# Head norms and memory softmax worked in place in PSUM, and an instruction index that goes back when a leading stream ends

## The chip, the cores and the metric

The kernel runs on one core of one Trainium2 chip. The metric is the device time of one execution in microseconds (us). Engines are named as in the profile: PE is the matrix engine (PEld its weight loads), DVE the vector engine, ACT the scalar engine, POOL the general-purpose engine, SP the engine that issues the transfers. SBUF is the working memory, PSUM the eight banks of 512 fp32 words per partition into which PE writes.

## The reference: two layers of a decoder trunk

Inputs are `x` (512 tokens of 1024), 256 memory tokens and the weights, all fp32. Each layer normalises `x`, projects it, runs three branches, gates them, concatenates them, projects back and adds.

```python
# layer 0:  A chunked spatial gating | B differential attention (8 heads x 2 maps of 32) | M memory attention
# layer 1:  C conformer convolution (31 taps) | D sparse attention (8 heads of 64, 2 groups) | M memory attention
q = rope_partial(rms_norm(q, qnorm), pos)        # per head: a "head norm", with or without rotation
def memory_attention(q, mem_n, w_kv, qnorm, knorm):
    k, v = jnp.split(mem_n @ w_kv, 2, axis=-1)
    q, k = rms_norm(q.reshape(..., 4, 64), qnorm), rms_norm(k.reshape(..., 4, 64), knorm)
    p = jax.nn.softmax(jnp.einsum('bshd,bmhd->bhsm', q, k) * 64 ** -0.5, axis=-1)
    return jnp.einsum('bhsm,bmhd->bshd', p, v)
```

## The kernel before

Tokens are cut into four tiles of 128. Products that need fp32 accuracy are made from two fp32r halves (high and low), three matmuls per product (`mm3`, L396 to L398). Each weight unit (128x1024) arrives by DMA, ACT writes its high half (`split`, L376) and POOL its low half (L377, POOL). Outputs that become matmul operands are split by ACT and DVE (L376, L377).

**Head norms.** `head_norm` (L488) serves memory queries and keys of both layers (`m_query`, `mem_kv`) and queries and keys of branch D (`d_q`, `d_kv`). The projection `p` lies in a PSUM bank. ACT squares it into the SBUF tile `sq`; DVE sums per head (L494); `rstd` takes two POOL instructions (L370, L372). Meanwhile DVE multiplies `p` by gain (L498) or gain times cosine (L501) into SBUF, over `sq`, makes the sine part `u` (L503) and adds it in two pieces (L504, L505). When `r` is there, `to_queries` multiplies by it in SBUF (L521) or `to_keys` does so into a doubled tile (L511), and PE transposes. `b_qk` does the same for branch B with its own lines (L873 to L883; L883 multiplies by `r`). From L504, L881, L511, L521 and L883 on, all tensors are in SBUF. Two token tiles of `b_qk`, and two of the layer-0 memory queries, share one PSUM bank; the others have a bank each.

**Memory softmax.** `m_attn` (L586) treats two heads at once, in one bank `s`: DVE takes the maximum (L600), ACT writes the exponentials to SBUF `e` (L603), DVE scales head 0 (L572) and POOL head 1 (L570) in place, PE transposes, ACT and DVE split, PE multiplies by the values (L582 to L584). There are 16 such steps, 8 in each layer.

**Compressed values and gates of D.** `d_cmp` copies a 64x64 PSUM result to SBUF by ACT (L1111) and spreads it with eight DVE copies (L1115); `m_q1` turns a tanh into a gate on DVE (L1134), once for each token tile.

**What sets the order.** The kernel emits all instructions once, and a scheduler at build time fixes each engine's queue: among the instructions that it holds ready it takes the one with the lowest index, and the index counts up as instructions are emitted. A block `high_priority(offset=n)` numbers its instructions from the current index minus n and at its normal end puts the index back, so that they use up no numbers. Streams are generators: `merge` interleaves a leading one with a filling one, and `ahead(g, n)` (L719) runs each step of the leading one in such a block. A generator that ends raises StopIteration inside the block. The block is then left by an exception, and the index isn't put back: it stays lower by n for all that follows. There are four leading streams: `m_attn` of layer 0 (n = 1000), `m_attn` of layer 1 (1000), `d_cmp` (100), `d_attn` (100). The convolution taps (`c_taps`, L1243; DVE L1260 and, for one channel tile, ACT L1257 with POOL L1258) are numbered 2000 higher than their place, so that they fill gaps; they read what `c_glu` projects (L1235, L1238). Dependences hold whatever the index. For PSUM they are kept by bank: a read of one half of a bank waits for a write of its other half that was emitted before it, and a write for such a read.

Banks and pages are handed out by the kernel at emission. Projections take banks of kind "d": six at first, three from the differential attention of layer 0 on, four in the projections of D.

## Time and profile before

| | |
|---|---|
| three timed runs | 733.96, 735.17 (median), 738.78 us |
| the profiled execution | 736.76 us |
| its span, first to last instruction | 734.7 us (2.06 us lie outside) |
| mean granted PE clock | 0.979 |
| busy: PE, PEld, DVE, ACT, POOL | 673.6, 571.1, 534.5, 366.9, 388.5 us |
| chain that ended last | PE 59%, DVE 23%, POOL 7%, ACT 4%, issue 4%, DMA 2% |

An engine's busy time is the time in which at least one of its instructions runs. A matmul's end is modelled and successive ones overlap, so a mean of 380 ns for one with 512 columns stands beside starts 227 ns apart. The stages of the span: start to 16 us, projections and head norms of B to 132, attention of B with its filling projections to 290, memory attention 0 and the output projection to 345, layer-1 norm to 361, memory queries, first channel tiles and memory attention 1 to 440 (its last products come at 480), projections of D to 545, attention of D to the end. The granted clock is given as a share of 2.4 GHz; 0.5 is 1.2 GHz.

### The profile page before, as it was taken

What the parts mean: (1) busy time and instruction counts of PE and PEld (TensorE: products, weight loads), DVE (VectorE), ACT (ScalarE), POOL (GpSimd) and SP (SyncE); (2) the same over time, 40 slices, a digit from 0 to 9 for tenths busy, and PEclk for the clock granted to TensorE, in tenths of its full rate; (3) what the DMA queues carried; (4) which work ended last, traced back from release to release, by engine and by line L of the source; (5) the groups of instructions that cost most, each with busy time, mean ns of one, the idle gap of its engine ahead of it and who ended that gap; (6) DMA issues with size and microseconds to landing.
All of it is one profiled execution on the core that took longest, in us unless ns stands there. A gap on an engine that the chain in (4) does not pass through costs nothing.

```text
span 734.7 us, 10935 instructions
## 1 busy us (share of the span) xinstructions
PE 673.6 (92%) x3819; PEld 571.1 (78%) x3819; DVE 534.5 (73%) x1216; ACT 366.9 (50%) x819; POOL 388.5 (53%) x343
## 2 busy tenths in 40 slices
PE   4999999999999888999899899698697989989997
PEld 3789998788899767888787777586586878777885
DVE  4607787767867788952749939997959678888773
ACT  5344354555464664732534466432425566665651
POOL 3376985554366469524647389963625233511450
PEclk9999999999999999999999999999898999999999
DMA  8542254643231435222223111022211011110121
GB/s 307 162 143 73 69 148 111 186 115 119 72 116 59 143 115 200 76 71 58 92 86 118 56 58 58 29 90 83 83 34 58 29 58 31 63 52 1 58 72 72
DMA packets 22375, 66.55 MB, mean 91 GB/s; under 512 B 3504, under 2 KB 3760, under 8 KB 22320
## 3 DMA queue, kind: packets, MB, share of 16 engines
q1 hardware_dynamic: 22320, 65.86, 27.4%
q8 instruction: 30, 0.49, 0.3%
q14 instruction: 25, 0.20, 0.1%
HBM read 57.46 MB, written 2.10 MB: 81 GB/s over the span
## 4 chain that ended last, share of the span: by engine, by line
PE 59%; DVE 23%; POOL 7%; issue 4%; ACT 4%; DMA 2%; SPq 0%; POOLq 0%; DVEq 0%; ACTq 0%
PE banks L396 15%; PE banks L397 15%; PE banks L398 15%; PE banks L393 5%; DVE banks L1260 4%; PE banks L923 3%; DVE arena_r L377 2%; POOL arena_f L372 2%; POOL arena_r L377 2%; DMA arena_f<-in_wall_dram 2%; PE banks L1211 2%; ACT arena_r L376 2%; DVE arena_f L925 2%; PE banks L961 1%; POOL arena_f L1258 1%
## 5 line engine op out<-in xcount | busy, mean ns | idle before, releaser
L396 PE MATMUL banks<-arena_r 128*128 128x512 f32 (+2 forms) x784 | 293.5, 380 | 13.9 <-DVE arena_f L473 3.3
L397 PE MATMUL banks<-arena_r 128*128 128x512 f32 (+2 forms) x784 | 292.2, 374 | 4.2 <-POOL arena_r L377 3.1
L398 PE MATMUL banks<-arena_r 128*128 128x512 f32 (+2 forms) x784 | 290.7, 373 | 0.6 <-POOL arena_r L377 0.5
L377 POOL TENSOR_TENSOR arena_r<-arena_f,arena_r 128x1024 fp32r<-128x1024 f32 (+2 forms) x87 | 211.2, 2436 | 143.9 <-ACT arena_r L376 141.3
L396 PEld LDWEIGHTS banks<-arena_r 128*128 128x128 f32 x784 | 150.6, 193 | 40.3 <-ACT arena_r L376 5.2
L397 PEld LDWEIGHTS banks<-arena_r 128*128 128x128 f32 x784 | 150.4, 192 | 28.0 <-POOL arena_r L377 4.0
L398 PEld LDWEIGHTS banks<-arena_r 128*128 128x128 f32 x784 | 150.1, 192 | 24.7 <-POOL arena_r L377 1.4
L376 ACT ACTIVATE arena_r<-arena_f 128x1024 fp32r<-128x1024 f32 (+2 forms) x131 | 110.4, 854 | 80.8 <-PE banks L398 19.3
L393 PE MATMUL banks<-const,arena_f 128*128 128x128 f32 x507 | 83.5, 281 | 28.0 <-DVE arena_f L411 9.6
L393 PEld LDWEIGHTS banks<-const,arena_f 128*128 128x128 f32 x507 | 62.6, 146 | 39.0 <-DVE arena_f L411 10.1
L377 DVE TENSOR_TENSOR arena_r<-banks,arena_r 128x512 fp32r<-128x512 f32 (+1 forms) x112 | 67.0, 608 | 26.1 <-ACT arena_r L376 25.6
L376 ACT ACTIVATE arena_r<-banks 128x512 fp32r<-128x512 f32 (+1 forms) x112 | 57.8, 532 | 43.9 <-PE banks L393 27.1
L925 DVE CUSTOM_DVE_ANT_0 arena_f<-banks,const 128x512 f32<-128x512 f32 (+3 forms) x128 | 60.2, 484 | 21.1 <-PE banks L923 15.1
L372 POOL TENSOR_TENSOR arena_f<-arena_f,const 128x4 f32<-128x4 f32 (+3 forms) x60 | 68.6, 1146 | 3.6
L570 POOL TENSOR_SCALAR arena_f<-arena_f 128x256 f32<-128x256 f32 (+3 forms) x48 | 29.0, 609 | 74.2 <-DVE arena_f L1190 25.2
L1260 DVE SCALAR_TENSOR_TENSOR banks<-arena_f,const,banks 128x482 f32<-128x482 f32 (+14 forms) x90 | 66.0, 733 | 1.4
L954 ACT ACTIVATE arena_f<-arena_f 128x512 f32<-128x512 f32 (+3 forms) x64 | 35.8, 560 | 45.8 <-DVE arena_f L925 45.4
L923 PE MATMUL banks<-arena_r 128*128 128x512 f32 (+7 forms) x192 | 51.5, 345 | 4.2 <-DVE arena_f L925 4.1
L653 DVE TENSOR_TENSOR arena_f<-arena_f,banks 128x512 f32<-128x512 f32 x40 | 27.3, 684 | 29.0 <-PE banks L398 28.3
L1188 ACT ACTIVATE arena_f<-arena_f 128x512 f32<-128x512 f32 (+3 forms) x64 | 35.6, 558 | 24.2 <-DVE arena_f L925 24.2
L370 POOL TENSOR_SCALAR arena_f<-arena_f 128x4 f32<-128x4 f32 (+3 forms) x60 | 19.0, 317 | 47.9 <-DVE arena_f L494 15.8
L923 PEld LDWEIGHTS banks<-arena_r 128*128 128x128 f32 (+1 forms) x192 | 33.1, 193 | 9.0 <-DVE arena_f L925 5.9
(175 smaller groups left out, 847.0 us busy)
## 6 DMA issues: line engine op xcount, KB each, us to landing
arena_f<-in_wall_dram SPq DMA_DIRECT2D x88, 512.0 KB, 3.3
arena_r<-arena_r SPq DMA_DIRECT2D x96, 64.0 KB, 2.0
arena_f<-in_x_dram SPq DMA_DIRECT2D x7, 512.0 KB, 4.6
arena_f<-in_w_dram SPq DMA_DIRECT2D x4, 512.0 KB, 3.9
out_dram<-arena_f SPq DMA_DIRECT2D x8, 256.0 KB, 2.0
arena_f<-in_norms_dram SPq DMA_DIRECT2D x3, 512.0 KB, 4.7
arena_f<-in_mem_dram SPq DMA_DIRECT2D x2, 512.0 KB, 3.2
arena_f<-in_wqb_dram SPq DMA_DIRECT2D x2, 420.0 KB, 3.3
```

The costliest lines, as they stand in the source:

```text
L372: G.tensor_tensor(r, v, mhalf[:parts, :n], ALU.pow)
L376: act(h, src, AF.Copy)
L377: (eng or V).tensor_tensor(l, src, f32(h), SUB)
L393: nc.tensor.transpose(o, i, ident[:k, :k])
L396: mm(o, lh, rh, start=first, stop=False)
L397: mm(o, lh, rl, start=False, stop=False)
L398: mm(o, ll, rh, start=False, stop=last)
L923: mm(t[:, a % per, :], q, k[:, :w], start=b == 0, stop=b == len(qk) - 1)
L925: V.tensor_tensor_reduce(e[a], t[:, a % per, :], cmask[:, S - w:], -1.0, -NEG, ADD, ALU.min, nm[:, a:a + 1])
L954: act(e[m], e[m], AF.Exp, bias=nm[:, m:m + 1], scale=-1.0, accum_out=l[:, i, m:m + 1])
L1188: act(es[j], es[j], AF.Exp, bias=nm[:, j:j + 1], scale=-1.0, accum_out=l[:, j:j + 1])
L1260: V.scalar_tensor_tensor(acc[:, z:], hc[:, :S - z], cw[:, f, k:k + 1], acc[:, z:], MUL, ADD)
```

## The change

All edits keep the arithmetic. In head norms the gain or cosine product and the two additions write over the projection in PSUM; `u` is made first; the multiplication by `r` reads PSUM and writes SBUF. In the memory softmax the exponentials overwrite the scores in PSUM; head 0 is scaled by DVE from PSUM to SBUF and head 1 by ACT instead of POOL. The spreading copies of `d_cmp` and the gate of `m_q1` go from DVE to ACT. `ahead` asks for the next step with a default, so that the block is left normally when the stream ends and the index goes back.

```diff
     def head_norm(sc, p, nh, gain, rope):
         act(sq, p3, AF.Square)
+        if rope is not None:
+            cg, sg = rope
+            u = sc([P, nh, 16])
+            V.tensor_tensor(u, p3[:, :, 0:16], bc(sg.unsqueeze(1), [P, nh, 16]), MUL)
         ss = sc([P, nh])
         V.tensor_reduce(ss, sq, AX.X, ADD)
         r = rstd(sc, ss, 1.0 / 64, nh)
-        t = sq
         if rope is None:
-            V.tensor_tensor(t, p3, bc(gain.unsqueeze(1), [P, nh, 64]), MUL)
+            V.tensor_tensor(p3, p3, bc(gain.unsqueeze(1), [P, nh, 64]), MUL)
         else:
-            cg, sg = rope
-            V.tensor_tensor(t, p3, bc(cg.unsqueeze(1), [P, nh, 64]), MUL)
-            u = sc([P, nh, 16])
-            V.tensor_tensor(u, p3[:, :, 0:16], bc(sg.unsqueeze(1), [P, nh, 16]), MUL)
-            V.tensor_tensor(t[:, :, 0:8], t[:, :, 0:8], u[:, :, 8:16], ADD)
-            V.tensor_tensor(t[:, :, 8:16], t[:, :, 8:16], u[:, :, 0:8], ADD)
-        return t, r
+            V.tensor_tensor(p3, p3, bc(cg.unsqueeze(1), [P, nh, 64]), MUL)
+            V.tensor_tensor(p3[:, :, 0:8], p3[:, :, 0:8], u[:, :, 8:16], ADD)
+            V.tensor_tensor(p3[:, :, 8:16], p3[:, :, 8:16], u[:, :, 0:8], ADD)
+        return p3, r, sq
...
-    def to_queries(sc, t, r, dst):
+    def to_queries(sc, q3, r, t, dst):
         nh = t.shape[1]
-        V.tensor_tensor(t, t, bc(r.unsqueeze(2), [P, nh, 64]), MUL)
+        V.tensor_tensor(t, q3, bc(r.unsqueeze(2), [P, nh, 64]), MUL)
...
                     for j in range(2):
-                        act(e[:, j, :], s[:, j, :], AF.Exp, bias=nm[:, j:j + 1], accum_out=l[:, j:j + 1])
+                        act(s[:, j, :], s[:, j, :], AF.Exp, bias=nm[:, j:j + 1], accum_out=l[:, j:j + 1])
                     V.reciprocal(l, l)
-                    for j in range(2):
-                        times(e[:, j, :], l[:, j:j + 1], SCALE_M[j])
+                    V.tensor_scalar(e[:, 0, :], s[:, 0, :], l[:, 0:1], None, MUL)
+                    act(e[:, 1, :], s[:, 1, :], AF.Copy, scale=l[:, 1:2])
...
     def ahead(g, n):
-        while n:
-            try:
-                with tc.high_priority(offset=n):
-                    c = next(g)
-            except StopIteration:
+        while True:
+            with tc.high_priority(offset=n):
+                c = next(g, None)
+            if c is None:
                 return
             yield c
-        yield from g
...
                 p4 = p.rearrange("p (j m d) -> p j m d", j=2, d=32)
-                V.tensor_tensor(t, p4, bc(bcg[:, i, :, :].unsqueeze(2), [P, 2, 4, 32]), MUL)
                 u = sc([P, 2, 4, 8])
                 V.tensor_tensor(u, p4[:, :, :, 0:8], bc(bsg[:, i, :, :].unsqueeze(2), [P, 2, 4, 8]), MUL)
-                V.tensor_tensor(t[:, :, :, 0:4], t[:, :, :, 0:4], u[:, :, :, 4:8], ADD)
-                V.tensor_tensor(t[:, :, :, 4:8], t[:, :, :, 4:8], u[:, :, :, 0:4], ADD)
-                V.tensor_tensor(t3, t3, bc(r.unsqueeze(2), [P, 8, 32]), MUL)
+                V.tensor_tensor(p4, p4, bc(bcg[:, i, :, :].unsqueeze(2), [P, 2, 4, 32]), MUL)
+                V.tensor_tensor(p4[:, :, :, 0:4], p4[:, :, :, 0:4], u[:, :, :, 4:8], ADD)
+                V.tensor_tensor(p4[:, :, :, 4:8], p4[:, :, :, 4:8], u[:, :, :, 0:4], ADD)
+                V.tensor_tensor(t3, p.rearrange("p (j d) -> p j d", d=32), bc(r.unsqueeze(2), [P, 8, 32]), MUL)
...
-                vs = sc([64, 64])
-                act(vs, o, AF.Copy, scale=0.5)
                 G.memset(cbd, 0.0)
                 for g in range(2):
                     for r in range(4):
-                        V.tensor_copy(cbd[32 * r:32 * r + 32, g, r, :], vs[32 * g:32 * g + 32, :])
+                        act(cbd[32 * r:32 * r + 32, g, r, :], o[32 * g:32 * g + 32, :], AF.Copy, scale=0.5)
...
                 act(th, p[:, 256:280], AF.Tanh, scale=0.5)
-                V.tensor_scalar(dgt[:, i, :, :].rearrange("p h b -> p (h b)"), th, 0.5, 0.5, MUL, ADD)
+                act(dgt[:, i, :, :].rearrange("p h b -> p (h b)"), th, AF.Copy, scale=0.5, bias=0.5)
```

`to_keys` changes only in its argument list: it reads the same product, now from PSUM.

## Rows read from the trace of the kernel before

**Rows 1.** The page, part 1: busy us (share of the span) and instructions.

```profile
PE 673.6 (92%) x3819; PEld 571.1 (78%) x3819; DVE 534.5 (73%) x1216; ACT 366.9 (50%) x819; POOL 388.5 (53%) x343
```

**Rows 2.** Windows: us, busy PE, PEld, DVE, ACT, POOL, then clock, DMA, GB/s.

```profile
240.00:300.00 60.00, 52.09 (x269) 43.28 (x268) 48.50 (x88) 35.42 (x84) 41.06 (x35) 0.97 0.42 142
380.00:440.00 60.00, 55.57 (x307) 46.20 (x306) 48.48 (x80) 31.14 (x72) 39.35 (x32) 1.00 0.25 87
420.00:440.00 20.00, 18.23 (x100) 14.73 (x100) 9.21 (x16) 12.24 (x26) 17.87 (x16) 1.00 0.15 53
500.00:545.00 45.00, 37.10 (x169) 29.86 (x170) 36.15 (x68) 16.03 (x34) 20.56 (x19) 0.89 0.17 55
```

**Rows 3.** Waits of PE: instruction <- releaser: us in total, times, longest.

```profile
PE banks L393 <- DVE arena_f L521: 5.9, 1, 5.9
...
PE banks L393 <- DVE arena_f L1160: 2.7, 1, 2.7
...
PE banks L396 <- DVE arena_f L498: 2.4, 1, 2.4
```

**Rows 4.** Single source lines on DVE: ns min/median/max, first and last start us.

```profile
L883 DVE TENSOR_TENSOR arena_f<-arena_f x16: 411/426/2589, 74.4 to 132.2; 128x256 f32<-128x256 f32 x16
...
L521 DVE TENSOR_TENSOR arena_f<-arena_f x12: 412/554/2659, 230.4 to 528.0; 128x256 f32<-128x256 f32 x8, 128x512 f32<-128x512 f32 x4
...
L498 DVE TENSOR_TENSOR arena_f<-banks,const x12: 408/416/425, 227.0 to 389.8; 128x256 f32<-128x256 f32 x12
```

**Rows 5.** Groups of instructions by line: busy us, mean ns | idle before.

```profile
L1260 DVE SCALAR_TENSOR_TENSOR banks<-arena_f,const,banks 128x482 f32<-128x482 f32 (+14 forms) x90 | 66.0, 733 | 1.4
...
L603 ACT ACTIVATE arena_f<-banks,arena_f 128x256 f32<-128x256 f32 x32 | 14.8, 473 | 20.4 <-DVE arena_f L600 20.2 <-DVE arena_f L604 0.2
...
L883 DVE TENSOR_TENSOR arena_f<-arena_f 128x256 f32<-128x256 f32 x16 | 14.0, 874 | 6.6 <-POOL arena_f L372 6.6
...
L521 DVE TENSOR_TENSOR arena_f<-arena_f 128x256 f32<-128x256 f32 (+1 forms) x12 | 13.4, 1120 | 0.5 <-POOL arena_f L372 0.4
...
L1115 DVE COPY const<-arena_f 32x64 f32<-32x64 f32 x8 | 3.7, 465 | 0.1
```

**Rows 6.** Timeline of DVE, last query norms of D: start us, us.

```profile
517.44 2.63 DVE L521 TENSOR_TENSOR arena_f<-arena_f 128x512 f32<-128x512 f32 x1
...
525.53 2.39 DVE L505 TENSOR_TENSOR arena_f<-arena_f 128x64 f32<-128x64 f32 x1
528.02 2.66 DVE L521 TENSOR_TENSOR arena_f<-arena_f 128x512 f32<-128x512 f32 x1
```

**Rows 7.** Timeline of POOL in the same stretch.

```profile
523.90 1.64 POOL L372 TENSOR_TENSOR arena_f<-arena_f,const 128x8 f32<-128x8 f32 x1
525.50 4.64 POOL L377 TENSOR_TENSOR arena_r<-arena_f,arena_r 128x1024 fp32r<-128x1024 f32 x2
```

**Rows 8.** Timeline of DVE at the start of D's attention.

```profile
551.24 3.82 DVE L1115 COPY const<-arena_f 32x64 f32<-32x64 f32 x8
...
560.61 2.31 DVE L1157 TENSOR_SCALAR arena_f<-arena_f 128x8 f32<-128x8 f32 x1
```

**Rows 9.** Window of line L572 on DVE (eight scalings of memory attention 1).

```profile
380.00:430.00 50.00, 7.26 (x8) 1.00 0.27 94
```

**Rows 10.** Timeline of DVE, memory keys of layer 1.

```profile
283.06 0.41 DVE L498 TENSOR_TENSOR arena_f<-banks,const 128x256 f32<-128x256 f32 x1
...
286.57 0.69 DVE L511 TENSOR_TENSOR arena_f<-arena_f 128x512 f32<-128x512 f32 x1
```

**Rows 11.** Timeline of DVE: input of the third channel tile of C.

```profile
440.90 0.69 DVE L1238 SCALAR_TENSOR_TENSOR arena_f<-arena_f,banks 128x512 f32<-128x512 f32 x1 [3.13 <-PE banks L398]
```

**Rows 12.** Timeline of DVE, one head norm of B.

```profile
89.90 0.21 DVE L880 TENSOR_TENSOR arena_f<-banks,const 128x64 f32<-128x64 f32 x1
...
95.39 2.59 DVE L883 TENSOR_TENSOR arena_f<-arena_f 128x256 f32<-128x256 f32 x1 [1.19 <-POOL arena_f L372]
```

**Rows 13.** A window of 5 us behind the wait for L521.

```profile
530.00:535.00 5.00, 4.26 (x15) 3.63 (x16) 3.71 (x8) 2.17 (x6) 2.87 (x5) 0.53 0.43 141
```

More of the change, by code (lines that the diff above doesn't have):

```diff
@@ L557, in mem_kv @@
             with SC() as sc:
-                t, r = head_norm(sc, p[:, 0:256], 4, mkg[layer], None)
-                to_keys(sc, t, r, kt[:, 0, :, tok(i)], kt[:, 1, :, tok(i)])
+                to_keys(sc, *head_norm(sc, p[:, 0:256], 4, mkg[layer], None), kt[:, 0, :, tok(i)], kt[:, 1, :, tok(i)])
             yield UT
@@ L564, in m_query @@
         with SC() as sc:
-            t, r = head_norm(sc, p, 4, mqg[layer], None)
-            to_queries(sc, t, r, [qs[:, :, tok(i)]])
+            to_queries(sc, *head_norm(sc, p, 4, mqg[layer], None), [qs[:, :, tok(i)]])
     def times(e, f, eng):
@@ L1039, in d_kv @@
             with SC() as sc:
-                t, r = head_norm(sc, p[:, 0:256], 4, None, (dcg[:, i, 1, :], dsg[:, i, 1, :]))
-                to_keys(sc, t, r, dkh[:, :, tok(i)], dkl[:, :, tok(i)])
+                to_keys(sc, *head_norm(sc, p[:, 0:256], 4, None, (dcg[:, i, 1, :], dsg[:, i, 1, :])), dkh[:, :, tok(i)], dkl[:, :, tok(i)])
             yield UT + 440
@@ L1046, in d_q @@
             with SC() as sc:
-                t, r = head_norm(sc, p, 8, None, (dcg[:, i, 0, :], dsg[:, i, 0, :]))
+                n = head_norm(sc, p, 8, None, (dcg[:, i, 0, :], dsg[:, i, 0, :]))
                 qsc = SC()
@@ L1050, in d_q @@
                 dqs[i] = (q, qsc)
-                to_queries(sc, t, r, [q[:, 0:4, :], q[:, 4:8, :]])
+                to_queries(sc, *n, [q[:, 0:4, :], q[:, 4:8, :]])
             yield UT + 880
@@ L1365 @@
 PTILE, WIDE = 1, 2
-SCALE_D, SCALE_M = "vp", "vp"
+SCALE_D = "vp"
 CD, CX = 80, 3600
```

2 lines of the change are left out of this document (1 added, 1 removed).

## The prediction

> **What bounds the kernel now.** I read the engine totals first. PE is busy 673.6 of 734.7 us [rows 1], so no change can gain more than the 61 us in which PE is idle, plus what a low clock costs; what a freed microsecond of DVE is worth depends on the stage. Next the windows: of the 61 us, 7.9 lie at 240 to 300 us and 4.4 at 380 to 440, and 7.9 at 500 to 545, where the clock is also down to 0.89 [rows 2]. In these three DVE is busy 80% of the time, and the low-priority taps fill what the norms leave. Then PE's own waits [rows 3]: one of 5.9 us for L521 (the query norms of D), one of 2.7 for L1160 (first softmax of D's attention) and one of 2.4 for L498 (a bank still being read). The first two end with DVE work that the change touches or that stands behind it.
>
> The line view shows why DVE is slow there. L883 and L521 have all operands in SBUF: their shortest take 0.41 us, their longest 2.59 and 2.66. L498, which reads PSUM, stays between 0.408 and 0.425 [rows 4]. Even a small addition, L505 with 64 elements, takes 2.39 us once [rows 6], and it and the L521 behind it fill just the time in which POOL does two splits, 525.50 to 530.14, 2.3 us each [rows 7]. So I read the excess as DVE waiting for POOL's SBUF access; L498 with its PSUM operand never does.
>
> **The change part by part.** *DVE instructions that move to PSUM.* The product by gain stays one PSUM read of 0.416 us [rows 4]; only its output moves. A PSUM-to-PSUM form of it isn't in the trace. The nearest is the tap L1260, in and out of PSUM, 0.733 us for 482 to 512 elements [rows 5], against 0.69 for 512 from SBUF undisturbed [rows 10]; so from nothing to 0.05 us each, 36 products, at most 2 us. I take 1. L883 falls from 874 ns to its undisturbed 426: 16 x 0.448 = 7.2 us of DVE. L521 falls from 13.4 us [rows 5] to 8 x 0.42 + 4 x 0.69 = 6.1: 7.3 us. The eight scalings of memory attention 1 cost 7.26 us [rows 9]; as PSUM reads of 0.42 they cost 3.4: 3.9 us. The eight copies L1115 leave DVE: 3.7 us [rows 5]. That is 22 us of DVE, and the additions, L511, L1134 and the scalings of layer 0 add some. Little of it is time: most of DVE's work lies beside a busy PE.
>
> The Trainium skill (page "SBUF — State Buffer", section "Who interferes with whom") says that a DVE instruction with two SBUF inputs contends with a GpSimd instruction that reads SBUF, and one with at most one SBUF input, outside the two-port modes, doesn't; by that rule the whole excess goes, which is the 22 us above, and the trace agrees [rows 4]. Its page "VectorE: DVE Perf Modes", section "Why PSUM operands drop a tier", speaks against one edit: a PSUM operand takes the faster mode from an fp32 tensor-scalar instruction. By it the undisturbed scalings get slower; the mean of the disturbed ones here is 0.91 us [rows 9], and 0.42 is less.
>
> *What is on the path.* First, at 530 us. DVE runs almost without a gap from 517.44 to 530.68: L521 2.63 us, then L505 2.39 and L521 2.66 [rows 6]. Undisturbed they take 0.69 [rows 10], at most the 0.42 of the wider L498, and 0.69: 5.9 us less, just PE's 5.9 us of waiting. What is late next is `rstd` of the last tile: POOL ends it at 525.54 [rows 7], so without moving that the product would end at 526.2 instead of 530.7, 4.4 us earlier; it moves a little, because its sum stood behind the first disturbed L521. Bounds 4.4 and 5.9; I take 5. Second, at 551 us. The copies L1115 hold DVE for 3.82 us [rows 8] ahead of the softmax that PE then waits 2.7 us for. On ACT they cost 8 copies at no more than the 0.473 of a 256-wide one, 3.8 us at the most, in a stretch where ACT is half idle; then L1157, disturbed itself (2.31 us), is what is late. Bounds 0 and 2.7; I take 2. Third, 380 to 440 us: some 4 us less of DVE in scalings [rows 9], and POOL loses the other eight. PE is idle 4.4 us there in all [rows 2], in waits of under 1 us; I take 2, bounds 0 and 4.4. Fourth, the clock: behind the 5.9 us wait PE ran at 0.53 for 5 us [rows 13], so 2.3 us of its work were lost at the lower level of 1.2 GHz. [...]
>
> *ACT.* It gets 16 scalings of about 0.47 us [rows 5], 8 copies, 4 gates: about 10 us on 366.9, in a queue busy half the time. Queued behind each scaling are splits that feed PE; a delay of 0.47 us per step stands against POOL's scaling, which had to wait for splits of 2.4 us. I cost it at nothing; if that cover fails, it is 8 x 0.47 = 3.8 us in memory attention 1.
>
> *What the in-place form costs: the bank is held longer.* Before, the bank of a projection is free after L503 or L880; now only after the product with `r`, behind POOL's `rstd`. In the norms of B that is from 90.11 (end of L880) to 97.98 (end of L883 of the same tile) [rows 12], 7.9 us, of which the disturbance of L883 itself is 2.2. The memory keys of layer 1 show a case that PE feels: PE waited 2.4 us for L498, which ended at 283.47 [rows 3, 10]; the product L511 of that tile starts at 286.57 and ends at 287.26. With nothing else to do PE would wait 3.8 us more. And two tiles or heads in one bank are now ordered by writes: the second tile's product must wait for the first tile's last read. Bounds 0 (other work fills in, since the scheduler knows of the wait) and 4 here, and 0 and 4 in the norms of B. I take 3 and 1.
>
> *The index.* Counting what the source emits: memory attention 0 ends at index 2585, and all that follows goes on from 1585; memory attention 1 ends at 2288, then 1288. So D's projections are numbered 1288 to 1656, ahead of the channel projections of C (2120 to 2288) that were emitted before them; in the changed kernel they come behind. The taps are numbered 3901 and more and stay last either way. In the trace the third channel tile has its input only at 440.90 [rows 11], and DVE is busy only 9.2 of 20 us before that [rows 2]: taps that were held up fall into D's projections. With the index put back these channel projections come first, D's later by as much, so PE's sum is the same. I cost it at 0, with bounds of 8 us either way: a gain if the taps are done before the last query norms, a loss if those norms come later by more than the taps save.
>
> *Sum against the profiled execution:* 736.8 - 5 - 2 - 2 - 1 + 1 + 3 + 1 + 0 = 731.8, with DVE's 1 us of dearer writes counted whole. Where the DVE time freed at 240 to 300 us (PE idle 7.9 there, L511 and L521 both disturbed) shortens that stretch too, I add a gain of 3, bounds 0 and 5: 728.8. The median of the runs is 1.6 us under the profiled one: 727.
>
> **The rivals.** *The freed time is not on the path (within 1%).* The waits at 530 and 551 shrink by their lower bounds, 4.4 and 0, the rest nothing, and the banks cost 3: 736.8 - 4.4 + 3 = 735.4, or 734 on the median's scale; up to the forecast it is a matter of degree, so I put its centre at 732. For it: PE is 92% busy. Against: the 5.9 us wait has nothing else in it.
>
> *Banks held (slower).* From the attention of B on there are three banks of kind "d". A pair of tiles of B fills one in 48 matmuls of 256 columns at about 0.12 us (half the 0.227 between starts of 512 columns), 5.8 us, so PE is back at it after 11.5 us, and a hold of 8 us is covered; with one of the three taken by a gate projection, it is back after 5.8, and a hold of 8 isn't. If four pairs of B, two of the memory queries and two key tiles each cost PE 2 to 3 us, that is about 20 us against gains of 10: 747 less 1.6, 745. It decides once more than four such waits show. The Trainium skill (page "PSUM — Partial Sum Buffer", section "PSUM bank collisions raise a hardware error") asks that accesses be guarded by bank, not by address; that is what orders the pair here, and what makes this 745. Against: the scheduler knows of these waits and can put other work in, and the disturbed 2.2 us of a hold go.
>
> *The order of C and D (faster still).* If the taps of the third tile start some 10 us earlier, the last norms meet no taps, and the waits of 500 to 545 us (7.9 idle, some 5 by the clock) go nearly whole: 728.8 - 8 = 721, or 719 on the median's scale. For it: DVE's gap. Against: the taps of one tile need one bank and follow each other.
>
> **How the numbers follow.** Forecast 727, chance 0.36; order of C and D 719, 0.10; within 1%, centre 732, 0.36; banks 745, 0.18. One per cent (7.35 us, 727.8 to 742.5) is about what a measurement of this kernel can tell from no change. Faster 0.46, same 0.36, slower 0.18. The range runs from 717, below the order case, to 744: it leaves out about half of the banks case and little else. The forecast's own range is 722 to 731.
>
> **What would show it.** L883 and L521 with no duration over 0.75 us, DVE about 25 to 30 us less busy, POOL 8 less, ACT 10 more; PE's wait for L521 at the end of D's queries under 1.5 us, the one for L1160 under 1. Banks: PE waits for L883, L521 or L511 on its first matmul of a projection, over 4 us in all. The order: L1238's third start well before D's first norm. I am wrong if DVE drops by 25 us and the span doesn't, or if an engine's new order opens waits in stages that the change doesn't touch.

## The result and the profile after

The changed kernel takes 718.02 us (median of four runs, 717.32 to 719.34) against 736.02 for the kernel before: ratio 0.974, 95% interval 0.9712 to 0.9767. It is 18 us faster, more than twice the 8 to 9 that were forecast; the range of 717 to 744 holds it, its own narrower range of 722 to 731 doesn't. The profiled execution took 717.62 us, its span is 715.9 us, 18.8 us shorter.

The page of the changed kernel, part 1, answers [rows 1]:

```profile
PE 671.8 (94%) x3819; PEld 571.8 (80%) x3819; DVE 516.8 (72%) x1204; ACT 376.0 (53%) x846; POOL 376.7 (53%) x327
```

DVE lost 17.7 us of busy time, POOL 11.8, ACT gained 9.1. PE did the same 3819 matmuls in nearly the same busy time; its pauses (the time in which no matmul runs) fell from 61.1 to 44.1 us. The changed kernel's source lines for the products with `r` (L879 is L883 before; ns min/median/max, first and last start us), which answer [rows 4], and for the scaling of head 0 (L603):

```profile
L879 DVE TENSOR_TENSOR arena_f<-banks,arena_f x16: 407/422/427, 74.6 to 135.4; 128x256 f32<-128x256 f32 x16
...
L521 DVE TENSOR_TENSOR arena_f<-banks,arena_f x12: 416/425/692, 236.5 to 517.3; 128x256 f32<-128x256 f32 x8, 128x512 f32<-128x512 f32 x4
...
L603 DVE TENSOR_SCALAR arena_f<-banks,arena_f x16: 471/484/485, 292.5 to 436.8; 128x256 f32<-128x256 f32 x16
```

None of these products is disturbed any more: the longest L521 went from 2.659 to 0.692 us. But the prediction named 25 to 30 us for DVE, and 17.7 came. Other DVE instructions with two SBUF inputs now lose more time beside POOL: one group of splits, before and after (busy us, mean ns | idle before), takes 9.2 us more, and a group of 32 in the attention of B (L957, now L953) 4.1 more.

```profile
L377 DVE TENSOR_TENSOR arena_r<-arena_f,arena_r 128x256 fp32r<-128x256 f32 x40 | 21.6, 561 | 5.8 <-ACT arena_r L376 5.8
L377 DVE TENSOR_TENSOR arena_r<-arena_f,arena_r 128x256 fp32r<-128x256 f32 x40 | 30.8, 794 | 5.0 <-ACT arena_r L376 4.1 <-PE banks L397 0.5
```

The changed kernel's waits of PE (instruction <- releaser: us in total, times, longest) answer [rows 3]:

```profile
PE banks L393 <- DVE arena_f L411: 9.9, 1, 9.9
...
PE banks L919 <- DVE arena_f L921: 3.8, 5, 1.1
...
PE banks L393 <- DVE arena_f L1153: 1.7, 1, 1.7
...
PE banks L396 <- DVE arena_f L511: 1.5, 2, 1.2
```

The wait of 5.9 us for L521 is gone, that for the first softmax of D (L1160 before, L1153 now) fell from 2.7 to 1.7, and the held bank of the memory keys shows as 1.5 us (L511) where L498 cost 2.4. These three lines make only 7.8 of the 17 us. The windows say where the rest is (us, busy PE, PEld, DVE, ACT, POOL, clock, DMA, GB/s); first the changed kernel:

```profile
240.00:300.00 60.00, 53.08 (x276) 44.10 (x275) 47.87 (x100) 39.39 (x94) 37.90 (x35) 0.94 0.44 150
...
380.00:440.00 60.00, 59.88 (x339) 51.50 (x339) 49.53 (x89) 39.24 (x88) 42.21 (x26) 1.00 0.29 97
440.00:500.00 60.00, 57.11 (x312) 46.88 (x311) 54.52 (x103) 27.46 (x47) 46.77 (x41) 0.95 0.21 71
500.00:545.00 45.00, 41.19 (x202) 32.36 (x201) 35.52 (x79) 22.30 (x53) 23.55 (x19) 0.99 0.18 59
545.00:580.00 35.00, 32.36 (x189) 26.97 (x188) 24.27 (x61) 19.74 (x44) 14.23 (x13) 1.00 0.09 31
```

and of the kernel before the windows that [rows 2] leaves out:

```profile
440.00:500.00 60.00, 52.74 (x290) 43.01 (x288) 54.63 (x97) 26.50 (x43) 47.09 (x39) 0.97 0.21 71
...
545.00:580.00 35.00, 31.16 (x155) 25.05 (x154) 27.04 (x68) 18.59 (x42) 15.50 (x12) 0.90 0.10 36
...
559.00:562.00 3.00, 1.25 (x10) 0.92 (x9) 2.91 (x5) 1.92 (x3) 1.97 (x2) 0.99 0.00 0
562.00:565.00 3.00, 1.04 (x3) 0.69 (x4) 2.87 (x7) 0.42 (x1) 0.89 (x1) 0.50 0.28 105
565.00:568.00 3.00, 3.00 (x9) 2.31 (x9) 2.63 (x10) 2.19 (x7) 1.53 (x3) 0.50 0.18 72
```

Between 440 and 500 us PE was idle 7.3 us before, in waits of 2.5 us and less that the prediction didn't count; 2.9 are left. Over the whole stage of the projections of D the pauses fell from 16.1 to 4.9. From 559 to 565 PE was idle 3.7 us, and from 562 on its clock stood at 0.50; the changed kernel's window of 545 to 580 us has 1.00.

**An account that closes.** For every kernel here, the span less the time in which PE is idle less the clock that was lost (each 3 us window's width times one minus its granted clock) leaves 656.7 to 660.1 us: 734.7 - 61.1 - 15.4 = 658.2 before, 715.9 - 44.1 - 13.6 = 658.2 after. PE's work is nearly a constant, and a kernel's time is that plus pauses plus lost clock. (A pause that falls into a stretch at the lower clock is counted in both: 2.5 us before, 1.0 after, at most 3.0. Without that the rest is 658.9 to 661.3.) So both can be summed by stage and compared between kernels whose work lies at different times. The stages end at events that each kernel has: the last memory query of layer 1 (here "layer 0", from 16 us on), the last maximum of memory attention 1 ("memory 1"), the first softmax of D ("projections of D", mostly d_kv and d_q), the last softmax of D ("attention of D"). Ahead of 16 us (9.0 to 10.5) and after the last softmax (5.5 to 6.3) the kernels hardly differ. Time and ratio beside pauses plus lost clock, in us:

```
kernel             time    ratio (95%)            layer 0  memory 1  proj. D  att. D   all
before             736.0   1                        18.5      3.5      22.9    16.3   76.5
after              718.0   0.974  (0.971-0.977)     25.5      0.1       8.3     8.4   57.7
e1_index           731.6   0.993  (0.991-0.996)     16.9      3.7      17.2    17.9   71.2
e2_norms           728.0   0.987  (0.981-0.993)     26.8      1.9      14.3    13.4   72.0
e3_softmax         732.4   0.995  (0.992-0.997)     19.8      2.0      22.4    14.2   73.9
e4_act             728.0   0.988  (0.984-0.993)     18.1      5.3      22.6     7.3   68.9
f2_no_l0           717.3   0.974  (0.969-0.979)     18.7      0.0      13.5    10.2   58.5
f3_no_index        716.0   0.972  (0.967-0.976)     24.0      0.1       7.3     7.1   53.9
f5_no_norms        712.7   0.968  (0.961-0.974)     18.8      1.7      12.9     3.5   53.2
f6_no_act          723.6   0.983  (0.977-0.988)     23.5      1.1       6.5    14.5   61.2
g1_fewtaps_before  736.7   0.999  (0.997-1.002)     18.2      3.5      22.1    16.3   75.0
g2_fewtaps_after   719.6   0.976  (0.973-0.979)     25.8      0.1       9.1    10.2   60.9
g3_soft_act        717.0   0.973  (0.970-0.976)     19.2      1.7      19.3     3.5   58.7
g4_lead300         712.2   0.967  (0.964-0.970)     23.9      0.1       4.7     6.4   50.3
h1_copies          723.1   0.981  (0.978-0.984)     19.6      3.5      23.3     3.5   64.8
h2_late_norms      721.9   0.979  (0.976-0.983)     19.4      1.9      10.3    14.8   61.9
h3_no_bqk          715.6   0.971  (0.968-0.974)     19.1      0.1       7.8    12.0   54.1
h4_late_lead300    716.3   0.971  (0.968-0.975)     17.1      0.0      11.4     8.7   53.5
k1_late_copies     711.3   0.965  (0.961-0.969)     19.1      0.2       8.7     8.5   52.2
k2_no_gates        714.9   0.969  (0.965-0.973)     21.4      1.3       6.1    10.2   54.7
```

The time is a median, but one execution stands behind the stages of each row. g4_lead300 and the changed kernel have the same order up to the attention of D, and their stages ahead of it still differ by 1.6 and 3.6 us; smaller differences between two rows mean nothing by themselves.

### The profile page after: what moved, and what is told of

Its sections match the earlier page's. It is cut to its first block, busy times and chain, and to the rows that moved or that the text cites. A ratio compares the mean times of both kernels' runs of the same rounds, so it can differ in the third digit from the quotient of the medians.

```text
span 715.9 us, 10912 instructions
## 1 busy us (share of the span) xinstructions
PE 671.8 (94%) x3819; PEld 571.8 (80%) x3819; DVE 516.8 (72%) x1204; ACT 376.0 (53%) x846; POOL 376.7 (53%) x327
## 4 chain that ended last, share of the span: by engine, by line
PE 76%; DVE 12%; ACT 4%; DMA 3%; POOL 3%; issue 2%; SPq 0%; ACTq 0%; DVEq 0%; POOLq 0%
PE banks L397 19%; PE banks L396 19%; PE banks L398 19%; PE banks L393 6%; PE banks L919 3%; DMA arena_f<-in_wall_dram 3%; ACT arena_r L376 2%; PE banks L957 2%; DVE arena_r L377 2%; PE banks L1204 2%; POOL arena_r L377 2%; DVE arena_f L921 2%; PE banks L1080 1%; PE banks L1174 1%; DVE banks L1253 1%
## 5 line engine op out<-in xcount | busy, mean ns | idle before, releaser
L376 ACT ACTIVATE arena_r<-arena_f 128x1024 fp32r<-128x1024 f32 (+2 forms) x131 | 110.3, 854 | 92.4 <-PE banks L398 22.4
L393 PE MATMUL banks<-const,arena_f 128*128 128x128 f32 x507 | 84.1, 282 | 21.6 <-DVE arena_f L411 9.9
L393 PEld LDWEIGHTS banks<-const,arena_f 128*128 128x128 f32 x507 | 62.4, 146 | 33.6 <-DVE arena_f L411 10.3
L921 DVE CUSTOM_DVE_ANT_0 arena_f<-banks,const 128x128 f32<-128x128 f32 (+3 forms) x128 | 60.1, 484 | 30.6 <-PE banks L919 23.1
L919 PE MATMUL banks<-arena_r 128*128 128x256 f32 (+7 forms) x192 | 50.7, 338 | 6.1 <-DVE arena_f L921 3.8
L950 ACT ACTIVATE arena_f<-arena_f 128x512 f32<-128x512 f32 (+3 forms) x64 | 35.6, 558 | 39.1 <-DVE arena_f L921 38.3
L568 POOL TENSOR_SCALAR arena_f<-arena_f 128x512 f32<-128x512 f32 (+3 forms) x32 | 21.3, 672 | 55.2 <-DVE arena_f L1183 40.2
L1181 ACT ACTIVATE arena_f<-arena_f 128x256 f32<-128x256 f32 (+3 forms) x64 | 35.6, 557 | 26.9 <-DVE arena_f L921 26.5
L370 POOL TENSOR_SCALAR arena_f<-arena_f 128x4 f32<-128x4 f32 (+3 forms) x60 | 15.9, 264 | 50.2 <-ACT arena_f L406 18.0
```

The lines of the kernel that those rows point to most:

```text
L376: act(h, src, AF.Copy)
L393: nc.tensor.transpose(o, i, ident[:k, :k])
L919: mm(t[:, a % per, :], q, k[:, :w], start=b == 0, stop=b == len(qk) - 1)
L921: V.tensor_tensor_reduce(e[a], t[:, a % per, :], cmask[:, S - w:], -1.0, -NEG, ADD, ALU.min, nm[:, a:a + 1])
L950: act(e[m], e[m], AF.Exp, bias=nm[:, m:m + 1], scale=-1.0, accum_out=l[:, i, m:m + 1])
L1181: act(es[j], es[j], AF.Exp, bias=nm[:, j:j + 1], scale=-1.0, accum_out=l[:, j:j + 1])
```

## The experiments

**The parts one by one.** Each is the kernel before with one part of the change. e1_index:

```diff
...
-            try:
-                with tc.high_priority(offset=n):
-                    c = next(g)
...
+            with tc.high_priority(offset=n):
+                c = next(g, None)
...
```

> The kernel before with the new ahead alone: the instruction index goes back when a leading stream ends; no arithmetic changes its engine or memory. Theory O (order): the projections of C now stand ahead of those of D, the third and fourth channel tiles get their input some 10 us earlier, and most of the 18 us appear here, 722 to 726 us. Theory P (port): the gain comes from DVE work that no longer waits for POOL; then this alone is 733 to 738, no change. Under either, the stretch up to the memory queries of layer 1 should stay within 2 us of before, since the leak of layer 0 reorders little there.

Measured 731.6 us, 4.5 less. The gain is in the projections of D (22.9 to 17.2): the last channel projection comes at 446.2 instead of 458.3 us. The time lies between the ranges of the two theories: order alone gives something, but not most of the 18 us.

e2_norms, all head norms with those of B:

```diff
-            V.tensor_tensor(t, p3, bc(cg.unsqueeze(1), [P, nh, 64]), MUL)
+            V.tensor_tensor(p3, p3, bc(cg.unsqueeze(1), [P, nh, 64]), MUL)
...
-        V.tensor_tensor(t, t, bc(r.unsqueeze(2), [P, nh, 64]), MUL)
+        V.tensor_tensor(t, q3, bc(r.unsqueeze(2), [P, nh, 64]), MUL)
```

> The kernel before with the head norms of all branches in place in PSUM, nothing else. Theory P: the disturbed products (28 us of DVE in all by the rows of before, about 15 of it in norms) go, PE's wait of 5.9 us at the last query norm shrinks to about 1, and the time is 724 to 729. Theory O: the path is set by the order, and this gives 733 to 738. Theory B (banks): the norms of layer 0 hold their banks longer; the layer-1 norm then starts 3 to 6 us later than before whatever the total does.

Measured 728.0 us, 8.0 less, as the difference of two larger amounts: 8 us lost in layer 0 and 13 gained behind it (of the profiled execution). Theory P named the time, and theory B holds beside it: the last instruction of the layer-1 norm starts at 368.6 instead of 361.4 us.

e3_softmax:

```diff
-                        act(e[:, j, :], s[:, j, :], AF.Exp, bias=nm[:, j:j + 1], accum_out=l[:, j:j + 1])
+                        act(s[:, j, :], s[:, j, :], AF.Exp, bias=nm[:, j:j + 1], accum_out=l[:, j:j + 1])
...
+                    V.tensor_scalar(e[:, 0, :], s[:, 0, :], l[:, 0:1], None, MUL)
+                    act(e[:, 1, :], s[:, 1, :], AF.Copy, scale=l[:, 1:2])
```

> The kernel before with the memory softmax in place in PSUM and head 1 scaled by ACT, nothing else. Theory P: 4 us of DVE and 4 us of POOL less in each memory attention, waits of PE between 400 and 440 us down by 1 to 3 us: 731 to 735. Theory O: no change, 733 to 738. If POOL's scalings were what held up the transposes of memory attention 1, its last products come at about 465 us instead of 480.

Measured 732.4 us, 3.7 less; memory attention 1 ends 7 us earlier (473.7 against 480.6), of which most is waited for again in the projections of D, which cost 22.4 against 22.9. The 4 us of DVE in each memory attention did not come: DVE is busy 536.1 us, where it was 534.5, as the splits shown above rose from 21.6 to 25.3 us while the disturbed scalings went. POOL lost 6.8.

e4_act, copies and gates on ACT:

```diff
-                vs = sc([64, 64])
-                act(vs, o, AF.Copy, scale=0.5)
...
-                        V.tensor_copy(cbd[32 * r:32 * r + 32, g, r, :], vs[32 * g:32 * g + 32, :])
+                        act(cbd[32 * r:32 * r + 32, g, r, :], o[32 * g:32 * g + 32, :], AF.Copy, scale=0.5)
...
-                V.tensor_scalar(dgt[:, i, :, :].rearrange("p h b -> p (h b)"), th, 0.5, 0.5, MUL, ADD)
+                act(dgt[:, i, :, :].rearrange("p h b -> p (h b)"), th, AF.Copy, scale=0.5, bias=0.5)
```

> The kernel before with the eight spreading copies of the compressed values and the four gates on ACT instead of DVE, nothing else. My prediction put 2 us on the copies: PE's wait of 2.7 us for the first softmax of D's attention goes, 732 to 734. If the copies were covered, no change, 734 to 737.

Measured 728.0 us, 8.1 less, all in the attention of D (16.3 to 7.3). I had put 2 us on it. By plain addition the four parts give 24.3 us; together they gave 18.

**One part left out of the changed kernel.** f2_no_l0 puts the norms of B, the memory queries of layer 0 and the memory keys of both layers back into SBUF:

```diff
-            to_queries(sc, *head_norm(sc, p, 4, mqg[layer], None), [qs[:, :, tok(i)]])
+            to_queries(sc, *(head_norm_s(sc, p, 4, mqg[0]) if layer == 0 else head_norm(sc, p, 4, mqg[layer], None)), [qs[:, :, tok(i)]])
```

(`head_norm_s` is the old form; `mem_kv` and `b_qk` likewise.)

> The changed kernel, but the head norms of branch B, of the memory queries of layer 0 and of the memory keys of both layers work in SBUF again, as before the change. Theory 'held banks': in the changed kernel the last instruction of the layer-1 norm comes 5.2 us later than before the change (366.6 against 361.4 us), because these norms hold their bank until the product with r; without that the layer-1 norm ends at 361 to 362 us again and the whole time falls by 3 to 6 us, to 712 to 715. Rival 'taken up later': the layer-1 norm comes back to 361 or 362 us, but layer 1 has its own limits and the whole stays within 716 to 720. Rival 'not the banks': the norm of layer 1 still ends at 365 us or later, since ACT's scalings or the softmax in place delay layer 0; the whole is 718 to 722.

Measured 717.3 us. Layer 0 recovers (25.5 to 18.7; the last instruction of the layer-1 norm starts at 363.3 us, against 366.6 in the changed kernel and 361.4 before), but the projections of D cost 5 us more: the rival, taken up later.

f3_no_index keeps the old `ahead` (e1's edit undone):

> The changed kernel with the old leading-stream helper, whose index isn't put back when a stream ends. Theory 'additive': the index alone gained 4.5 us on the kernel before, so leaving it out costs as much, 722 to 724 us, and the taps of the third channel tile and its copy end at about 520 us instead of 509. Rival 'needed by the others': the norms in PSUM and the index meet in the projections of D; leaving the index out costs 8 us or more, 726 and up. Rival 'redundant': once DVE is relieved the order hardly matters, and the time is 717 to 720.

Measured 716.0 us, no slower than with it: redundant, and with it the theory of additive parts falls. f5_no_norms leaves all norms in SBUF (e2's edit undone):

> The changed kernel with all head norms in SBUF, as before the change (softmax, index and the work moved to ACT stay changed). Theory 'additive': the norms alone gained 8.0 us, so leaving them out costs as much, 725 to 727 us; the layer-1 norm ends at about 361 us, and the last query product of D at some 520 us or later, with single products of 2 us or more. Rival 'order had already cured it': with the index put back the last norms of D meet no taps; the time is 716 to 720. Rival 'held banks outweigh': without the held banks of layer 0 the time is 712 to 716.

Measured 712.7 us. The norms, worth 8 us alone, bring nothing beside the other three parts, and by the medians cost 5. f6_no_act leaves copies and gates on DVE (e4's edit undone):

> The changed kernel with the eight spreading copies of the compressed values and the gates of D on DVE again, as before the change. Theory 'additive': these two alone gained 8.1 us on the kernel before, so leaving them out costs about 8 us, 725 to 727. Rival 'as large as the wait in front of it': they are worth what the trace of before shows at the first softmax of D, 2 to 3 us, and the 8 us came with a reordering that the other parts bring too; 719 to 721.

Measured 723.6 us, between the two ranges: of the three parts left out, the one without which the changed kernel is clearly slower. Its attention of D costs 14.5 us again. The softmax was not left out by itself, so what it is worth beside the other three is not known.

**Is DVE's amount of work the limit?** g1_fewtaps_before and g2_fewtaps_after leave out every second tap of one channel tile:

```diff
-            for k in range(30):
+            for k in range(0, 30, 2 if f == 3 else 1):
```

> The kernel before, but for the last of the three channel tiles whose convolution runs on DVE every second tap is left out: 15 of 30 instructions of 0.735 us, 11.0 us less work on DVE, none less on PE, and the result for those channels is wrong by the missing taps. Theory 'DVE sets the pace': from the end of memory attention 1 to the first softmax of D the kernel before needs DVE's time, 98 us in a stage of 125, of which 45 are taps, and whatever is taken from DVE there comes off the time; 725 to 729 us. Rival 'single waits': taps have the lowest priority and only fill gaps, so the time falls by no more than the part of the 5.9 us wait that they cause, 0 to 3 us; 732 to 736.

> The changed kernel with the same 15 taps left out (11.0 us less of DVE's work, the same missing terms in the result). Theory 'DVE sets the pace, until it no longer does': in the changed kernel PE is idle only 4.9 us from memory attention 1 to the first softmax of D, so there is little left to gain; 714 to 717 us, a gain well under that of the same cut in the kernel before. Rival 'still DVE': the gain is the same 8 us or more, 707 to 710.

Measured 736.7 and 719.6 us: 11 us less of DVE's work gains nothing in either. In g1 the taps are done 26 us earlier (their last copy at 496.0 instead of 521.7 us), and PE waits for L521 all the same:

```profile
PE banks L393 <- DVE arena_f L521: 5.0, 1, 5.0
```

Its DVE timeline (start, us) at that wait:

```profile
524.04 2.40 DVE L505 TENSOR_TENSOR arena_f<-arena_f 128x64 f32<-128x64 f32 x1
526.54 2.66 DVE L521 TENSOR_TENSOR arena_f<-arena_f 128x512 f32<-128x512 f32 x1
```

and POOL's:

```profile
524.01 4.64 POOL L377 TENSOR_TENSOR arena_r<-arena_f,arena_r 128x1024 fp32r<-128x1024 f32 x2
```

With no tap near, the addition of 64 elements and the product behind it take the 5 us in which POOL does two splits, as in [rows 6, 7]. So it is the length of the norm's own chain that PE waits for, not how much else DVE does.

**Which two parts suffice.** g3_soft_act has the softmax in PSUM and the work moved to ACT (e3's and e4's edits), nothing else:

> The memory softmax in PSUM and the copies and gates on ACT, without the norms in PSUM and without the index put back: of the four parts the two that only take work from DVE and POOL. Theory 'relief alone': these two bring nearly all of it, 711 to 716 us, as leaving out the index cost nothing in the changed kernel and leaving out the norms gained 5. Rival 'one of the two others is needed': with the norms in SBUF the disturbed norms of D come on the taps again unless the index goes back; 719 to 725. By plain addition of the separate gains it would be 736 - 3.7 - 8.1 = 724.

Measured 717.0 us: as fast as the whole change. Separately these two gained 3.7 and 8.1, together 20.4; here the sum is too small. g4_lead300 is the changed kernel with one number altered:

```diff
-HM0, HM1, HD, HC = 1000, 1000, 100, 100
+HM0, HM1, HD, HC = 1000,1000,300,100
```

> The changed kernel with one number altered: the attention of D is numbered 300 instead of 100 ahead of the work that fills beside it. The work is the same to the instruction, only its order after the first softmax of D differs. It measures what order alone is worth there, since the kernel without the norms in PSUM needs 169 us from the first softmax of D to the end and the changed one 179. Theory 'order decides the rest': the time moves by 3 us or more, either way; below 715 or above 721. Rival 'order is nothing': 717 to 719.

Measured 712.2 us: 6 us by order alone. So differences of up to some 6 us between kernels can come from the order that the scheduler happens to find, and f5's advantage over the changed kernel is of that size. So are the gains of the single parts, 3.7 to 8.1 us, each of which came with another order too; what an edit does is read from the stage and the wait that it was to change, and from several kernels with and without it.

**Copies, late norms and early norms apart.** h1_copies is the kernel before with only the first half of e4's edit, the copies:

> The kernel before with only the eight spreading copies on ACT; the gates stay on DVE. Theory 'copies': of the 8.1 us that copies and gates gained together, all comes from the copies, which in the kernel before stretch the first softmax of D from 5.4 to 12.9 us and leave PE at 0.50 of its clock behind it; 727 to 729 us, clock 1.00 in the 10 us after the first softmax. Rival 'gates too': the gates, early in layer 1, shift the order of what follows; 730 to 735 with the copies alone.

Measured 723.1 us, 14.6 less, more than any of the four parts alone. It is all in the attention of D, 16.3 to 3.5 us. Its window there, beside that of the kernel before above:

```profile
545.00:580.00 35.00, 34.80 (x184) 27.93 (x183) 27.53 (x76) 23.07 (x56) 16.51 (x14) 1.00 0.16 53
```

PE is idle 0.2 us instead of 3.8, and no clock is lost instead of 3.5 (0.10 of 35). The other 5.7 us come later in that stage. The copies themselves, on DVE in the kernel before and on ACT here (ns min/median/max):

```profile
L1115 DVE COPY const<-arena_f x8: 184/186/1373, 551.2 to 554.9; 32x64 f32<-32x64 f32 x8
L1113 ACT ACTIVATE const<-banks x8: 212/214/215, 550.8 to 552.3; 32x64 f32<-32x64 f32 x8
```

They take 1.8 us in all, where DVE took 3.82 [rows 8]. DVE's undisturbed copy is no slower, 0.186 us; two of its eight were held up beside POOL, one for 1.373 us. h2_late_norms is the kernel before with only the norms of D and the memory queries of layer 1 in PSUM (e2's edit with f2's exception):

> The kernel before with only the head norms of D and of the memory queries of layer 1 in PSUM; those of branch B, of the memory queries of layer 0 and the memory keys stay in SBUF. All norms together gained 8.0 us, while the layer-1 norm ended 7.2 us later. Theory 'a gain behind a loss': without the held banks of layer 0 the gain of D's norms is whole, 11 to 14 us, so 722 to 725. Rival 'taken up later': what layer 0 doesn't lose is waited for in layer 1, the time stays at 727 to 729. Rival 'the wait for L521 alone': 5 us, 730 to 732.

Measured 721.9 us, 15.8 less: a gain behind a loss. The projections of D cost 10.3 us instead of 22.9. Its key product, L511 of the kernel before, stands at line 521 here, and shows the two forms side by side: four from SBUF (the memory keys of both layers) and four from PSUM (the keys of D), each 512 wide:

```profile
L521 DVE TENSOR_TENSOR arena_f<-arena_f x4: 682/1246/2889, 268.0 to 290.1; 128x512 f32<-128x512 f32 x4
L521 DVE TENSOR_TENSOR arena_f<-banks,arena_f x4: 685/686/691, 457.6 to 483.1; 128x512 f32<-128x512 f32 x4
```

h3_no_bqk is the changed kernel with B's norms alone back in SBUF (the hunk of `b_qk` undone):

> The changed kernel with the norms of branch B alone back in SBUF; those of the memory and of D stay in PSUM. Where do the 6 us that layer 0 loses (pauses of PE and low clock up to the memory queries of layer 1) come from? Theory 'memory keys': they stay, pauses and lost clock from 16 us to the last memory query of layer 1 sum to 23 to 25 us as in the changed kernel, with a wait for L511 in 270 to 300 us. Rival 'branch B': they go, 18 to 20 us. The whole time 716 to 720 in either case.

Measured 715.6 us; layer 0 has 19.1 us of pauses and lost clock instead of 25.5. The rival was right: it is branch B that loses there. Over all kernels: with B's norms in PSUM 23.5 to 26.8 (six), with only the memory's early norms 19.1 and 21.4, with none 16.9 to 19.8 (twelve).

h4_late_lead300 joins f2's and g4's edits, k1_late_copies f2's exception with the gates back on DVE, k2_no_gates h3's exception with the gates on DVE:

> The changed kernel without the early norms in PSUM (branch B, memory queries of layer 0, memory keys) and with the attention of D 300 ahead: the two edits by which the changed kernel still seemed to lose. If the stages add up, 6 us of layer 0 come back and 5 us of D's attention: 707 to 711 us, under both kernels and under all runs so far. Rival 'given back': layer 1 takes up again what layer 0 gains, as when these norms alone were put back (717.3); 711 to 714, no better than the lead of 300 by itself (712.2).

> All parts of the change but two: the early norms (branch B, memory queries of layer 0, memory keys) are in SBUF, and the gates of D are on DVE, both as before the change. Copies alone gained 14.6 us, D's norms alone 15.8. If the stages add up, D's attention keeps 3.5 us of pauses and lost clock as with the copies alone, layer 0 keeps its 18 to 19, and the stretch from memory attention 1 to the first softmax of D falls to 8 to 13: 705 to 710 us, under both kernels. Rival 'a floor': what one part frees is taken up again by the next limit, 711 to 716 as in the other good combinations.

> The changed kernel without the norms of branch B in PSUM and with the gates of D on DVE; it differs by the gates alone from the run without branch B's norms, which took 715.6 us. Theory 'the gates on ACT cost': with them on DVE the pauses and lost clock of D's attention fall from 12 to some 4 us, 707 to 711 us. Rival 'the order in D's attention has another cause': 714 to 717.

Measured 716.3, 711.3 and 714.9 us. In the first what layer 0 gave back was paused for again in D. In k2 the attention of D comes down to 10.2 us from h3's 12.0 and not to 4, so beside the other parts the gates on ACT cost nothing that shows. e4 and h1 differ by the gates alone and by 5 us; that this is order is likely but not shown. k1 has the lowest median, 711.3 (708.9 to 713.8, ratio 0.961 to 0.969, all of it below the changed kernel's interval), but f5, g4 and k2 are no further off than their intervals. Copies and late norms gained 14.6 and 15.8 alone, and 26.7 with the rest of k1: several edits remove the same pauses, and the kernels settle at about 50 us of pauses and lost clock, some 15 of them at the two ends.

Several times fell outside every range that was named for them by 1 us or more: e1, f6 and g3 between their ranges, e4 and h1 faster, g2 and h4 slower. For these the readings above rest on the stages and waits, not on a theory's number.

## Why the prediction was right or wrong

Its sum against what the stages show, before to after (pauses plus lost clock, us): layer 0 +7.0, memory attention 1 -3.4, projections of D -14.6, attention of D -7.9, both ends 0; -18.8 in all against -8 forecast. The sum had put +1 on layer 0 (banks +3 and +1, 240 to 300 us -3) and -10 on what follows (-5, -2, -2, -1); the stages show +7.0 and -25.9. The two errors cancel in part, and that the wide range still holds 718 is luck to that extent.

**The query norms of D, -5, and the stretches around them.** Right in mechanism: [rows 6, 7] read the excess as DVE waiting for POOL's access to SBUF; h2 shows one product with and without it in one kernel (the keys', up to 2.889 us from SBUF, 0.691 from PSUM), and g1 excludes the taps as its cause. The Trainium skill (page "SBUF — State Buffer", section "Who interferes with whom") says the same of a DVE instruction with two SBUF inputs beside a GpSimd (here POOL) instruction that reads SBUF, and the trace agrees: 2.659 us at most before, 0.692 after. The whole trace says the same: in the kernel before none of 566 DVE instructions with a PSUM input lasted more than 0.04 us longer than the shortest of its line and form, while 49 of 609 without one lasted over 0.4 us longer, up to 2.2, each with POOL at work for at least as long as the excess (groups of three or more). No run takes POOL's work away instead. The size failed, because I listed windows of 240 to 300, 380 to 440 and 500 to 545 [rows 2] and passed over 440 to 500, where PE was idle 7.3 us. The step that failed is costing a stage by its longest waits: of the 16.1 us of pauses in the projections of D I counted 5.9, and 10 more lay in pieces of 0.5 to 2.5, and behind them, at 473 and 504 us, the clock fell too, for 1.7 us of lost clock each time. Most of these pieces end with a split or with the gating of the memory heads (L578), none with an instruction of a norm; the norms that stand among them, D's keys, lost 1.8 us, in the addition L504. h2, the norms there alone, took 12.6 us off the stage, 7.5 of pauses and 5.1 of lost clock; so the norms do shorten these pieces, but by which steps wasn't traced.

**The copies, -2, bounds 0 and 2.7.** The term that was mis-sized most. I took PE's wait for L1160 as the most that could go. The eight copies lay inside the first softmax of D; in the 6 us from 559 to 565 PE was idle 3.7 us, and from 562 until past 568 its clock stood at 0.50. h1 put their worth at 12.8 us in that stage: 7.1 at the place itself (3.6 of pause and 3.5 of clock, of which 1.0 is counted in both), the rest further on in pauses and one more stretch at the lower clock, which I haven't traced; part of it may be order. In the changed kernel, with another order, they are worth less: without copies and gates on ACT (f6) the stage costs 6.1 us more. The bound was wrong in kind: a wait that the profile shows is not the ceiling, since what it costs in clock and what then comes late is not in its row.

**380 to 440 us, -2.** Nearer its upper bound of 4.4: the stage fell from 3.5 to 0.1. e3 gives about half of that to the softmax (3.5 to 2.0; f5 and g3, which have it without the norms, stand at 1.7), and e2 and h2 the rest to the norms (1.9).

**The clock, -1.** No run shows this 1 as a term of its own. What the runs showed in its place: lost clock fell from 15.4 to 13.6 us, right in size but only as a sum, since projections and attention of D gave back 8.5 and layer 0 lost 6.8 more.

**Banks held, +3 and +1.** The sum, 4, was low against 7, and stood at the wrong place. The memory keys, which I took for the worse, cost at most some 2, within what two executions differ by (19.1 and 21.4 against a mean of 18.6 in the twelve kernels without), and PE's wait for their bank, 1.5 us, is shorter than before. The norms of B, which I took at 1, cost about 5. Nor is it the wait that I described: in the changed kernel the pauses of layer 0 sum to 15.2 us, against 15.0 before, and no wait for L879 is left; what rose is the lost clock, 3.4 to 10.2 us. The pauses lie at other places, and alike ones have unlike sequels: after a pause of 1.6 us at 362 us the changed kernel's clock fell (0.63 from 364 to 367 us), after one of 2.4 us at 281 us the clock before stayed at 1.00. How the hold leads there wasn't settled; the step that failed is taking its price to be PE's wait for the bank.

**240 to 300 us, -3.** It didn't come: 1 us less of pauses, and 1.8 us more of lost clock (0.97 to 0.94 of 60).

**The index, 0 with 8 either way.** Alone it gains 4.5 us, and the order moved as I had counted it out: the last channel projection starts 12 us earlier. Beside the other parts it gains nothing (f3). The rival "order of C and D" named 719, close to what was measured, but f3 reaches 716 without that order, so its mechanism isn't what made the time.

**Dearer writes in PSUM, +1.** Too high for the products: L501 from PSUM to PSUM takes 0.423 us as against 0.416 before, and the additions lost their disturbance. The scaling of head 0 takes 0.484 us from PSUM; undisturbed in SBUF its shortest was 0.339. The Trainium skill (page "VectorE: DVE Perf Modes", section "Why PSUM operands drop a tier") has that order, and the measured numbers agree; the mean of the eight in memory attention 1 was 0.91 [rows 9], so each of these still gains. DVE as a whole gained less than forecast: the 22 us of the prediction, which count the 3.7 of the copies as excess, came as 17.7, because the excess moved in part to other instructions; summed as above over those without a PSUM input it fell from 83.7 to 57.5 us, and in e3 alone it did not fall at all (84.5).

**ACT, 0.** It took 9.1 us more and no part shows a loss by it; k2 against h3 shows none for the gates. What I said would show the steps was seen for L521 and L883, for PE's wait at L521 and for the banks (under 4 us); not for DVE (17.7 less, 25 to 30 named), and the wait at the first softmax stayed at 1.7 where I had named under 1.

What stays open is the attention of D. With the copies on ACT its pauses and lost clock lie between 3.5 and 12 us (13.4 to 17.9 with them on DVE), and g4 shows that order moves the whole time by 6 us; which order is good was not found out.

## What to carry to other kernels

Take the kernel's time apart into PE's constant work, its pauses and the clock that it lost, by stages that end at events, and do it over the whole span: many small pauses in a stage that looks busy can weigh more than the longest wait. Price an edit on the critical chain by the pause it leaves and by the low clock and the late work behind it, not by the wait's row alone. And where edits remove the same pauses, measure each one left out as well as alone: here the four gained 24 us apart and 18 together, and two of them gave the same 717. Last, an instruction taken off a contended path hands its waits to the others there: look at the engine's whole busy time, not at the instruction alone.

## What the runs showed of the hardware

DVE instructions with a PSUM input were never held up: over the twenty kernels none lasted more than 0.07 us longer than the shortest of its line and form, while those without one lasted up to 2.25 us longer, always with POOL at work for as long as the excess. A copy of 32x64 took ACT 0.214 us from PSUM and DVE 0.186 from SBUF to the same place, but up to 1.373 beside POOL. While PE paused for 3.7 us between 559 and 565 us, its granted clock went to 0.50 of 2.4 GHz, that is to the lower level, at 562 us and stayed there until past 568; without the pauses (h1) it stayed at 1.00. Even with the same order, single executions differed by up to 3.6 us in the pauses and lost clock of one stage, and over all kernels the sum of PE's work at full clock stayed within 3.4 us.
